# A hybrid decoder block on one core: mixer weight sums at other steps, the fifth product's sums through two buffers, feed-forward sums on GpSimd

## The chip, the core and the metric

The kernel runs on one core of a Trainium2 chip. The core has a matrix engine (TensorE, PE in the profile; PEld is its loading of weights), a vector engine (VectorE, DVE), a scalar engine (ScalarE, ACT), a general engine (GpSimd, POOL) and SyncE (SP), which here issues nearly all transfers between DRAM and the on-chip memory SBUF. TensorE writes its results into PSUM banks. Every engine works through its own list of instructions in a fixed order, and an instruction waits on semaphores until its operands are there. An instruction that waits holds up all that stands behind it on its engine, transfers that SP issues included.

The metric is the device time of one execution in microseconds (us).

## What is computed

The block works on 1024 tokens of width 1024, in float32. A state-space branch and an attention branch read one normalised input, are gated and merged, and go through one output projection. Then come a cross-attention into 256 memory tokens, a SwiGLU feed-forward part of hidden width 2816, and a last norm.

```python
u = rms_norm(h, norm_mix[l])
proj = u @ w_in[l]
...
h = h + (gate_a * out_a + gate_b * out_b) @ w_mix_out[l]
h = h + memory_cross_attention(rms_norm(h, norm_mem_q[l]), rms_norm(mem, norm_mem_kv[l]),
                               w_mem_q[l], w_mem_kv[l], w_mem_o[l])
f_a, f_b = jnp.split(rms_norm(h, norm_ffn[l]) @ w_ffn_in[l], 2, axis=-1)
h = h + (jax.nn.silu(f_a) * f_b) @ w_ffn_out[l]
return rms_norm(h, norm_final)
```

The change touches the projection by `w_mix_out` and the product by `w_ffn_in`, with the weights prepared for the first while the state-space branch runs.

## The kernel before

Every matmul operand is held as two rounded parts, high and low. `B.split` (L177, L178) makes them: ScalarE copies the source to the high part, and VectorE (or GpSimd, where its last argument says so) subtracts to get the low part. A product of two such operands is three matmuls per step: high by high, high by low, low by high.

Large products are done by a seven-product scheme on 2 x 2 blocks: instead of eight block products there are seven, of sums of blocks. The operands of the left side are named A11, A12, A22 (blocks) and S1 to S4 (sums of blocks); the weights' sums are made in the same way. A name with h or l at the end is a high or low part: S4h, S4l.

The text names three places in the program.

**The state-space stage** (`stage_ssm`) runs a list of 32 gate products, `gates`, and hangs other work on their numbers through the dictionary `todo`. Four groups of states, q = 0 to 3, hang on gates 4 + 7q and the following ones: `turn_weights`, `states`, `toeplitz` (a strip built by doubling in the buffer Ts), `out`. xg is the load of the states' input from DRAM. On the same list hang the sums of the mixer weights, k = 0 to 3: `mix_fetch` loads two row blocks of `w_mix_out` into two buffers mw, `mix_sums` makes four sums on VectorE (L501), and `mix_store` writes them to the DRAM array sums_d (L505). Before the change these three hang on gates 7k, 7k + 2 and 7k + 3.

**The mixer** (in `stage_tail`) runs seven products by n in the order 1, 2, 6, 5, 3, 7, 4, each in four row groups `mix_mm(n, i)`, and adds each result into the hidden rows H (`mix_add`, L622, the tiles h in the profile). So product 5, with operand S1, is the fourth in this order, and product 3, with operand S4, is the fifth. The sums S4 lie in DRAM (s_d in the profile). `mix_s4(kk)` loads one half into a buffer with the tag xs, of which there is one, and `give` splits it into S4h and S4l. Beside the products a list `side` prepares the first two panels of the feed-forward weights: wpr is the raw panel, wph and wpl its high and low part, and the sums between them are made on GpSimd (L694 to L699). The gain of the next norm is spread over the partitions by `bcast_gain` into a buffer gbc, of which there is one too. `scaled` scales a token block for that norm: the sum of squares, `rsqrt` with a power on GpSimd (L196), its refinement rt and r on VectorE (L200 to L202), and xs = h x r x gain (L216).

**The feed-forward start.** `norm_blocks(t)` does the same for the eight token blocks t = 0 to 7, turns the scaled block with TensorE (L222, into banks misc and pv), and makes the operands. For t below 4 the turned block is stored to x_d and split into A11 and A12. For t = 4 to 7 the stored block comes back as xa, ScalarE copies the second half to sx, and VectorE makes s (for S3), the first half of sx (for S1), then two more sums in xa (L880 for S2, L881 for S4). `put` splits S2, S3 and S1; the fourth sum and A22 go to r_d and come back in `norm_rest` as xr. The products of the first panels, `start(0)`, `start(1)`, `middle(0)` and so on, call `prod` (L962). The second panel's `start(1)` uses A11 and A12 with weights whi and wlo from w_d; the first that reads S2 is `middle(0)`.

A scheduler with a cost model puts every engine's instructions in order when the program is built, so that the order of the lists is not that of the code.

Of the kernel before, what the change touches and what calls it, by code (L numbers as in the profile page):

```python
# [9 lines left out]
F32 = mybir.dt.float32  # L10
# [4 lines left out]
ALU = mybir.AluOpType  # L15
# [4 lines left out]
P = 128  # L20
D = 1024
# [435 lines left out]
def stage_ssm(B, s5, qp, uT, w_in, gate_d, u_d, y_d, w_mix_out, sums_d):  # L457

    A, S = B.A, B.S
    s5.qp = qp  # L460
    w = {}

    def gate_weights(p):

        w[p] = [B.wblock(w_in, 4 * n, 4, C_G + 256 * p, 256) for n in range(2)]

    def gate(j, h):
        if h == 0 and j % 2 == 0 and j < 14:
            gate_weights(j // 2 + 1)
        ps = B.bank()  # L470
        o = j % 2 * P
        for k in range(8):
            wh, wl = [t_[:, k % 4, o:o + P] for t_ in w[j // 2][k // 4]]
            B.mm3(ps, wh, wl, *uT.rhs(k, h), k == 0, k == 7)
        gs = qp.tile([P, 512], F32, tag="gs", bufs=2, name="gs")
        mark.append(A.activation(gs, ps, AF.Sigmoid))
        A.dma_start(gate_d[j * P:(j + 1) * P, 512 * h:512 * h + 512], gs)

    def toeplitz():
        with B.tc.issue_after(mark[-1].ins):  # L480
            s5.toeplitz()

    def weights(q):
        with B.tc.issue_after(s5.doubled.ins):
            s5.weights(q)

    mw = {}

    def mix_fetch(k):
        mw[k] = [qp.tile([P, D], F32, tag="mw", bufs=2, name="mw") for _ in range(2)]  # L490
        for w_, r_ in zip(mw[k], (k, 4 + k)):
            S.dma_start(w_, w_mix_out[r_ * P:(r_ + 1) * P, :])

    def mix_parts(k):
        (b11, b12), (b21, b22) = [(w_[:, :512], w_[:, 512:]) for w_ in mw[k]]
        return (5, b11, b12), (7, b12, b22), (6, b22, b11), (4, b21, b22)

    def mix_sums(k):

        for _, o, i in mix_parts(k):  # L500
            B.V.tensor_add(o, o, i)  # L501

    def mix_store(k):
        for n, o, _ in mix_parts(k):
            S.dma_start(sums_d[n, k // 2][:, k % 2 * 512:k % 2 * 512 + 512], o)  # L505

    mark = []
    gates = [lambda j=j, h=h: gate(j, h) for j in range(16) for h in range(2)]
    gate_weights(0)
    s5.weights(0)  # L510
    todo = {}
    for q in range(4):
        todo[4 + 7 * q] = [lambda q=q: s5.turn_weights(q)]
        todo[5 + 7 * q] = [lambda q=q: s5.states(q, u_d)] + ([lambda q=q: weights(q + 1)] if q < 3 else [])
        todo[8 + 7 * q] = [toeplitz]
        todo[9 + 7 * q] = [lambda q=q: s5.out(q), lambda q=q: s5.store(q, y_d)]
    for k in range(4):
        for i, f in ((7 * k, mix_fetch), (7 * k + 2, mix_sums), (7 * k + 3, mix_store)):
            todo.setdefault(i, []).append(lambda f=f, k=k: f(k))
    for i, f in enumerate(gates):  # L520
        for g in todo.get(i, []):
            g()
        f()


def stage_tail(B, big, s2, sh, x, glu, aT, gate_d, kv_d, sums_d, w_fox_o, w_mix_out, g_mq, w_mem_q, w_mem_o, g_ffn,
               w_ffn_in, w_ffn_out, g_fin, out):
    nc, V, A, G, T, S, small, ident = B.nc, B.V, B.A, B.G, B.T, B.S, B.small, B.ident
# [18 lines left out]
    fox, part, xm, mixw, msets, late = {}, {}, {}, {}, [], []  # L547
# [6 lines left out]
    def give(name, mk, k, src):  # L554
        B.split(*[a[k // 2][:, k % 2, :] for a in operand(name, mk)], src)
# [93 lines left out]
    H = [bslot(name=f"h{t}") for t in range(NT)]  # L649
    for t in range(NT):  # L650
        S.dma_start(H[t], x[t * P:(t + 1) * P, :])
    gq = B.bcast_gain(s2, g_mq)
    u2 = Act(s2, "t", NS2, 8, L, name="u2")

    xss = {}

    def scaled(t):
        xss[t] = tmp("xs")
        B.norm_scale(xss[t], H[t], B.rstd(H[t]), gq)

    def turned(t, banks):
        B.norm_turn(xss.pop(t), u2, t, banks)
# [54 lines left out]
        return [fetch, plain, sums, seventh, rest]  # L717

    def mix_s4(kk):
        y = s2.tile([P, D], F32, tag="xs", bufs=1, name="s4")  # L720
        S.dma_start(y, s3_d[kk])
        for k in range(2):
            give("S4", bslot, 2 * kk + k, y[:, 512 * k:512 * k + 512])

    side = [f for j in range(AHEAD_IN) for f in ahead(j)]
    side[6:6] = [lambda kk=kk: mix_s4(kk) for kk in range(2)]
    mix_weights(6)
    for i in range(4):
        mix_add(1, i)
    for n, m in ((2, 5), (6, 3), (5, 7), (3, 4), (7, None), (4, None)):  # L730
        for i in range(4):
            mix_mm(n, i)
            if n == 7:
                turned(i, ("mm", "misc"))
            mix_add(n, i)
            if n in (3, 4):
                scaled((n == 4) * 4 + i)
            elif late:
                late.pop()()
            elif side:  # L740
                side.pop(0)()
        if m:
            mix_weights(m)

# [101 lines left out]
            comb[name] = [[mk(F32R, f"{name}{s}").rearrange("p (k c) -> p k c", k=2) for _ in range(2)] for s in "hl"]  # L846
        return comb[name]

    def put(name, mk, i, src, neg=False):

        hi_, lo_ = blocks(name, mk)
        for kk in range(2):
            sv = src[:, kk * 256:(kk + 1) * 256].rearrange("p (k c) -> p k c", k=2)
            hi, lo = [a[kk][:, :, i * P:(i + 1) * P] for a in (hi_, lo_)]
            if neg:
                A.activation(hi, sv, AF.Copy, scale=-1.0)
                V.scalar_tensor_tensor(out=lo, in0=sv, scalar=-1.0, in1=f32(hi), op0=ALU.mult, op1=ALU.subtract)
            else:
                B.split(hi, lo, sv)

    def norm_blocks(t):
        i = t % 4
        xs = s2.tile([P, D], F32, tag="xs", bufs=1, name="xs")
        B.norm_scale(xs, H[t], B.rstd(H[t]), gf)
        S.dma_start(h_d[t], H[t])
        ps = [B.turn(xs, b, ("misc", "pv")[b]) for b in range(2)]
        if t < 4:
            for b in range(2):
                xf = sh.half("xf")
                A.copy(xf, ps[b])  # L870
                S.dma_start(x_d[i][:, 512 * b:512 * b + 512], xf)
                put(("A11", "A12")[b], slot, i, xf)
            return
        xa, sx, s3 = tmp("xa"), tmp("sx"), sh.half("s3")
        S.dma_start(xa, x_d[i])
        a11, a12, s1n, a22 = xa[:, :512], xa[:, 512:], sx[:, :512], sx[:, 512:]
        A.copy(a22, ps[1])
        V.tensor_sub(s3, a11, ps[0])
        V.tensor_sub(s1n, ps[0], a22)
        V.tensor_sub(a11, s1n, a11)  # L880
        V.scalar_tensor_tensor(out=a12, in0=a11, scalar=-1.0, in1=a12, op0=ALU.mult, op1=ALU.subtract)  # L881
        put("S2", slot, i, a11)
        put("S3", bslot, i, s3)
        put("S1", bslot, i, s1n, neg=True)
        S.dma_start(r_d[i][:, :512], a12)
        S.dma_start(r_d[i][:, 512:], a22)

    def norm_rest(i):
        y = tmp("xr")
        S.dma_start(y, r_d[i])  # L890
        put("S4", bslot, i, y[:, :512])
        put("A22", bslot, i, y[:, 512:])

    raws, wts, ev = {}, {}, {}
# [163 lines left out]
    for j in range(2, NF):  # L1058
# [7 lines left out]
        f = w_fetch(j + 2) if j + 2 < NF else f  # L1066
# [840 lines left out]
```

## Time and profile before

| | us |
|---|---|
| runs | 1604.41, 1609.55, 1599.38 |
| median of the runs | 1604.41 |
| profiled execution, its own time | 1599.39 |
| span of the profiled execution | 1597.6 |
| mean granted TensorE clock | 0.981 of full |

A row of a timeline reads: start in us, length in us, engine, line, operation, output<-input, shapes, and how often in a row; in square brackets stands the idle time of the engine before it and what ended it. A row of the waits reads: engine and line that waited, what it waited for, then us in total, times, longest us. SPq is SyncE's queue issuing transfers.

The stages that the change touches lie, by the names in the timeline, from 130 to 200 us (the first group of states), from 750 to 805 us (the mixer's last products) and from 940 to 975 us (the feed-forward start).

### The profile page before, as it was taken

To read this page: it belongs to the slowest core of one execution; us is meant where nothing else is said; L and a number is where in the kernel's file an instruction comes from. 1 tells how busy PE (TensorE), PEld (TensorE's weight loads), DVE (VectorE), ACT (ScalarE), POOL (GpSimd) and SP (SyncE) were. 2 spreads that over 40 slices of the span, in tenths; PEclk is the share of its full clock that TensorE was granted. 3 is DMA by queue.
4 is the path that set the end of the run, shared out by engine and by line. 5 is a ranking of instruction groups with operands and counts; after the bars stand their busy time and mean duration, and the time that the engine had idled before them with its cause. 6 is when DMAs were issued, how large, how long until landed. Compare 5 with 4: busy or idle time off the path is not lost.

```text
span 1597.6 us, 20547 instructions
## 1 busy us (share of the span) xinstructions
PE 1533.2 (96%) x7301; PEld 1260.2 (79%) x7301; DVE 1069.6 (67%) x1886; ACT 671.1 (42%) x1191; POOL 266.1 (17%) x337
## 2 busy tenths in 40 slices
PE   5899899999999899999899989999999999999997
PEld 5688788898777668887688778888888888788885
DVE  5757666435687777778775687777677776565455
ACT  5522343422566554223455565333333333344342
POOL 3014434110121123213201200010000000000001
PEclk8899999999999999999999999999999999999998
DMA  8747745652032736557732177445544554796642
GB/s 268 147 95 172 229 124 103 135 175 31 1 68 43 164 101 184 198 178 279 243 105 93 53 262 271 158 156 161 168 156 152 162 161 148 278 391 212 196 152 106
DMA packets 202872, 258.71 MB, mean 162 GB/s; under 512 B 36025, under 2 KB 127065, under 8 KB 202257
## 3 DMA queue, kind: packets, MB, share of 16 engines
q1 hardware_dynamic: 196144, 241.67, 50.3%
q10 hardware_dynamic: 6624, 15.73, 2.6%
q8 instruction: 57, 0.93, 0.2%
q14 instruction: 47, 0.38, 0.1%
HBM read 176.08 MB, written 83.20 MB: 162 GB/s over the span
## 4 chain that ended last, share of the span: by engine, by line
PE 78%; DVE 8%; DMA 5%; POOL 3%; issue 3%; ACT 2%; SPq 1%; DVEq 0%; ACTq 0%; POOLq 0%
PE mm L962 15%; PE pv L962 7%; PE mm L167 7%; PE mm L168 7%; PE mm L169 7%; PE mm L1099 4%; PE sc L962 4%; PE sc L1099 3%; PE pv L1099 3%; PE sc L167 2%; PE sc L169 2%; PE sc L168 2%; PE misc L1099 1%; PE pv L167 1%; PE pv L169 1%
## 5 line engine op out<-in xcount | busy, mean ns | idle before, releaser
L178 DVE TENSOR_TENSOR wlo<-raw,whi 128x1024 fp32r<-128x1024 f32 (+2 forms) x126 | 134.8, 1072 | 113.9 <-ACT whi L177 113.5
L177 ACT CAST whi<-raw 128x1024 fp32r<-128x1024 f32 (+2 forms) x127 | 115.6, 914 | 140.7 <-PE mm L168 43.6
L167 PE MATMUL mm<-uh,whi 128*128 128x512 f32 x344 | 139.6, 406 | 1.9 <-ACT whi L177 1.8
L169 PE MATMUL mm<-uh,wlo 128*128 128x512 f32 x344 | 137.0, 399 | 0.5 <-DVE wlo L178 0.5
L168 PE MATMUL mm<-ul,whi 128*128 128x512 f32 x344 | 137.1, 398 | 0.0
L178 DVE TENSOR_TENSOR ol<-or,oh 128x1024 fp32r<-128x1024 f32 x73 | 89.4, 1224 | 70.8 <-ACT oh L177 69.6
L177 ACT CAST oh<-or 128x1024 fp32r<-128x1024 f32 x73 | 76.8, 1053 | 103.4 <-PE mm L1099 34.9
L994 POOL TENSOR_TENSOR g<-a,c 128x512 f32<-128x512 f32 x22 | 35.6, 1618 | 392.6 <-ACT a L993 392.6
L1726 POOL TENSOR_TENSOR pl<-pf,ph 128x512 fp32r<-128x512 f32 (+1 forms) x32 | 39.5, 1234 | 244.7 <-DVE ph L1725 198.1
L169 PEld LDWEIGHTS mm<-uh,wlo 128*128 128x128 f32 x344 | 66.0, 192 | 15.2 <-DVE wlo L178 1.5
L167 PEld LDWEIGHTS mm<-uh,whi 128*128 128x128 f32 x344 | 66.4, 193 | 14.6 <-ACT whi L177 2.3
L168 PEld LDWEIGHTS mm<-ul,whi 128*128 128x128 f32 x344 | 66.2, 193 | 11.2
L196 POOL TENSOR_TENSOR r<-ms,mhalf 128x1 f32<-128x1 f32 (+1 forms) x30 | 20.6, 690 | 309.2 <-DVE ms L192 280.4
L1723 ACT ACTIVATE pf<-sc 128x512 f32<-128x512 f32 (+1 forms) x96 | 46.5, 490 | 48.5 <-DVE sc L1719 28.6
L962 PE MATMUL pv<-S3h,we 128*128 128x512 f32 x176 | 58.1, 389 | 0.0
L1729 DVE TENSOR_TENSOR pl<-pf,ph 128x512 fp32r<-128x512 f32 (+2 forms) x64 | 35.6, 558 | 10.5 <-ACT ph L1728 9.4
L1099 PE MATMUL mm<-ol,oh 128*128 128x512 f32 x106 | 41.2, 389 | 0.0
L1099 PE MATMUL mm<-oh,ol 128*128 128x512 f32 x106 | 41.2, 389 | 0.0
L1099 PE MATMUL mm<-oh 128*128 128x512 f32 x106 | 41.2, 389 | 0.0
L1194 POOL TENSOR_TENSOR sg<-sg,ga 128x512 f32<-128x512 f32 x16 | 28.8, 1821 | 72.8 <-DVE sg L1187 72.8
L167 PE MATMUL mm<-yh,whi 128*128 128x512 f32 x104 | 40.9, 393 | 0.0
L167 PE MATMUL sc<-uh,whi 128*128 128x512 f32 x104 | 40.8, 393 | 0.0
(680 smaller groups left out, 4610.7 us busy)
## 6 DMA issues: line engine op xcount, KB each, us to landing
or<-c_d SPq DMA_DIRECT2D x77, 256.0 KB
wo<-in_w_ffn_out_dram SPq DMA_DIRECT2D x22, 512.0 KB
c_d<-g SPq DMA_DIRECT2D x44, 256.0 KB
t_d<-wo SPq DMA_DIRECT2D x44, 256.0 KB
or<-t_d SPq DMA_DIRECT2D x44, 256.0 KB
raw<-in_w_ffn_in_dram SPq DMA_DIRECT2D x20, 512.0 KB
rawb<-in_w_ffn_in_dram SPq DMA_DIRECT2D x20, 512.0 KB
raw<-in_w_in_dram SPq DMA_DIRECT2D x18, 512.0 KB
```

Of the source, the lines that this page charges most:

```text
L167: T.matmul(ps, lh, rh, start=first, stop=False)
L168: T.matmul(ps, lh, rl, start=False, stop=False)
L169: T.matmul(ps, ll, rh, start=False, stop=last)
L177: self.A.copy(hi, src)
L178: (self.G if pool_lo else self.V).tensor_sub(lo, src, f32(hi))
L962: T.matmul(ps, l_[:, k, :], r_, start=first and k == 0 and i == 0, stop=k == 3 and i == 2, skip_group_check=True)
L994: G.tensor_mul(g[:, 512:], a1, c1)
L1099: T.matmul(ps, l_[:, gi], r_[:, 512:], start=n < 3 and p == 0 and k == 0 or n == 7 and p == 0 and k == 0, stop=p == NP - 1 and k == 2, ski ...
L1194: self.B.G.tensor_mul(self.out[j][:, cs], self.out[j][:, cs], ga)
L1723: self.exp = A.activation(pf[:, off:], ps[:, off:], AF.Exp)
L1726: G.tensor_sub(pl[:, off:], pf[:, off:], f32(ph[:, off:]))
L1729: V.tensor_sub(pl[:, off:], pf[:, off:], f32(ph[:, off:]))
```

## The change

1. `mix_fetch`, `mix_sums` and `mix_store` hang on gates 10 + 5k, 12 + 5k and 13 + 5k instead of 7k, 7k + 2 and 7k + 3.
2. The two halves of S4 are loaded into two buffers, with the tags xs and gbc, and their parts go to `slot` buffers (those that A11 had for the first product) instead of `bslot`. The pieces in `late` and the two loads are now the head of the list `side`. The gain of the norm, which uses gbc, is loaded after product 6.
3. In `norm_blocks`, for t = 4 to 7, the third and fourth sums are made on GpSimd. The fourth is a plain addition, and its sign is put right later, where S4 is split with `neg=True`. S2 is split last, and its low part on GpSimd.

```diff
-        for i, f in ((7 * k, mix_fetch), (7 * k + 2, mix_sums), (7 * k + 3, mix_store)):
+        for i, f in ((10 + 5 * k, mix_fetch), (12 + 5 * k, mix_sums), (13 + 5 * k, mix_store)):
...
-    gq = B.bcast_gain(s2, g_mq)
...
-    xss = {}
+    xss, gq = {}, []
...
-        B.norm_scale(xss[t], H[t], B.rstd(H[t]), gq)
+        B.norm_scale(xss[t], H[t], B.rstd(H[t]), gq[0])
...
-        y = s2.tile([P, D], F32, tag="xs", bufs=1, name="s4")
+        y = s2.tile([P, D], F32, tag=("xs", "gbc")[kk], bufs=1, name="s4")
...
-            give("S4", bslot, 2 * kk + k, y[:, 512 * k:512 * k + 512])
+            give("S4", slot, 2 * kk + k, y[:, 512 * k:512 * k + 512])
...
-    side[6:6] = [lambda kk=kk: mix_s4(kk) for kk in range(2)]
+    side[:0] = late + [lambda kk=kk: mix_s4(kk) for kk in range(2)]
...
-            elif late:
-                late.pop()()
             elif side:
                 side.pop(0)()
+        if n == 6:
+            gq.append(B.bcast_gain(s2, g_mq))
...
-    def put(name, mk, i, src, neg=False):
+    def put(name, mk, i, src, neg=False, low=V):
...
-                B.split(hi, lo, sv)
+                B.split(hi, lo, sv, low is G)
...
-        V.tensor_sub(a11, s1n, a11)
-        V.scalar_tensor_tensor(out=a12, in0=a11, scalar=-1.0, in1=a12, op0=ALU.mult, op1=ALU.subtract)
-        put("S2", slot, i, a11)
+        G.tensor_sub(a11, s1n, a11)
+        G.tensor_add(a12, a11, a12)
         put("S3", bslot, i, s3)
         put("S1", bslot, i, s1n, neg=True)
+        put("S2", slot, i, a11, low=G)
...
-        put("S4", bslot, i, y[:, :512])
+        put("S4", bslot, i, y[:, :512], neg=True)
```

How the scheduled order moves, at three places. The lines of the changed kernel are one lower than before from L653 on. First SP's list in the state-space stage. Before, from the last two u_d stores of the projection on:

```order
L440 DMA u_d<-us 128x8x128
L153 DMA raw<-in_w_in_dram 128x4x256
L492 DMA mw<-in_w_mix_out_dram 128x1024 x2
L1450 DMA xg<-u_d 128x1024
L505 DMA sums_d<-mw 128x512 x3
L492 DMA mw<-in_w_mix_out_dram 128x1024
L505 DMA sums_d<-mw 128x512 x2
L492 DMA mw<-in_w_mix_out_dram 128x1024
L153 DMA raw<-in_w_in_dram 128x4x256 x2
L1439 DMA Ts<-Ts 112x128
```

The changed kernel from the same place:

```order
L440 DMA u_d<-us 128x8x128
L153 DMA raw<-in_w_in_dram 128x4x256
L1449 DMA xg<-u_d 128x1024
L492 DMA mw<-in_w_mix_out_dram 128x1024 x2
L505 DMA sums_d<-mw 128x512 x4
L492 DMA mw<-in_w_mix_out_dram 128x1024 x2
L153 DMA raw<-in_w_in_dram 128x4x256
L505 DMA sums_d<-mw 128x512
L153 DMA raw<-in_w_in_dram 128x4x256
L1438 DMA Ts<-Ts 112x128
```

The first xg load has moved ahead of the first two fetches, and the fourth store of the first group ahead of the second group's fetches. From the copy of Ts with 96 partitions on, SP's list is the same in both.

Second, VectorE's list in the mixer, from the first panel's wpl on to the first h of the fifth product's successor. The rows h<-h,mm and h<-h,misc at the start are the sums of product 5. Before:

```order
L178 TENSOR_TENSOR wpl<-wpr,wph 128x1024
L178 TENSOR_TENSOR S4l<-s_7202,S4h 128x512 x2
L622 TENSOR_TENSOR h_6964<-h_6964,mm 128x512
L622 TENSOR_TENSOR h_6965<-h_6965,mm 128x512
L178 TENSOR_TENSOR wpl<-wpr,wph 128x512
L178 TENSOR_TENSOR wph<-wpr,wph 128x512
L622 TENSOR_TENSOR h_6966<-h_6966,misc 128x512
L178 TENSOR_TENSOR wlo<-raw,whi 128x1024
```

The changed kernel:

```order
L178 TENSOR_TENSOR wpl<-wpr,wph 128x1024
L622 TENSOR_TENSOR h_6964<-h_6964,mm 128x512
L622 TENSOR_TENSOR h_6965<-h_6965,mm 128x512
L178 TENSOR_TENSOR wpl<-wpr,wph 128x512
L178 TENSOR_TENSOR wlo<-raw,whi 128x1024
L178 TENSOR_TENSOR wpl<-wpr,wph 128x512
L622 TENSOR_TENSOR h_6966<-h_6966,misc 128x512
```

The two S4l have left this place (all four now stand together ahead of product 5's sums), and the sum of the misc bank has moved behind a weight split and behind the second wpl of 128x512. On SP, the load of the gain now stands between the two loads of product 3's weights, ahead of the next panel's wpr.

Third, GpSimd's list at the feed-forward start. r_8941, r_9024 and r_9075 are the powers for the token blocks t = 5, 6 and 7. Before, with the end of the list of norms and what follows:

```order
L196 TENSOR_TENSOR r_8854<-ms_8853,mhalf 128x1
L196 TENSOR_TENSOR r_8941<-ms_8940,mhalf 128x1
L196 TENSOR_TENSOR r_9024<-ms_9023,mhalf 128x1
L196 TENSOR_TENSOR r_9075<-ms_9074,mhalf 128x1
L994 TENSOR_TENSOR g<-a_9222,c_9248 128x512
```

The changed kernel:

```order
L196 TENSOR_TENSOR r_8941<-ms_8940,mhalf 128x1
L879 TENSOR_TENSOR xa<-sx,xa 128x512
L196 TENSOR_TENSOR r_9024<-ms_9023,mhalf 128x1
L880 TENSOR_TENSOR xa<-xa 128x512
L178 TENSOR_TENSOR S2l<-xa,S2h 128x2x128 x2
L879 TENSOR_TENSOR xa<-sx,xa 128x512
L880 TENSOR_TENSOR xa<-xa 128x512
L178 TENSOR_TENSOR S2l<-xa,S2h 128x2x128 x2
L196 TENSOR_TENSOR r_9075<-ms_9074,mhalf 128x1
L879 TENSOR_TENSOR xa<-sx,xa 128x512
```

The groups of t = 4 and t = 5 now stand among the powers, that of t = 5 ahead of the power for t = 7; the groups of t = 6 and t = 7 follow. On TensorE the turns of t = 7 into pv have moved directly behind those of t = 6, and its turns into misc behind the first product of the second panel.

## The prediction

> **What bounds the kernel now.** I read the page first, then TensorE's waits over the whole span, then windows around them, and last the timelines of the engines that these waits name. The page:
>
> ```profile
> span 1597.6 us, 20547 instructions
> PE 1533.2 (96%) x7301; PEld 1260.2 (79%) x7301; DVE 1069.6 (67%) x1886; ACT 671.1 (42%) x1191; POOL 266.1 (17%) x337
> ```
>
> TensorE is busy for 1533.2 of 1597.6 us, so 64.4 us are idle, and no part of the change removes a matmul. All that the change can win is idle time of TensorE and the slow clock behind it. Its waits, longest first where the change touches them:
>
> ```profile
> PE mm L615 <- ACT S4h L177: 3.5, 1, 3.5
> PE misc L222 <- DVE rt L201: 3.1, 1, 3.1
> PE pv L1426 <- ACT m L1504: 2.3, 1, 2.3
> PE pv L1500 <- ACT Tt L1444: 2.0, 1, 2.0
> PE misc L222 <- DVE u2l L178: 1.2, 1, 1.2
> PE misc L222 <- DVE h L622: 1.0, 1, 1.0
> PE mm L962 <- DMA whi<-w_d: 0.9, 1, 0.9
> PE mm L615 <- DVE S4l L178: 0.7, 1, 0.7
> PE pv L1457 <- DMA xg<-u_d: 0.7, 1, 0.7
> ```
>
> L1426, L1500 and L1457 are the first group of states (5.0 us), S4h and S4l are the fifth product (4.2), rt and whi the feed-forward start (4.0). The windows give the clock behind them (columns: window, length, busy time of PE, PEld, DVE, ACT and POOL with counts, granted clock, DMA share, GB/s):
>
> ```profile
> 190.00:193.00 3.00, 3.00 (x11) 2.52 (x11) 2.97 (x4) 0.96 (x2) 2.42 (x4) 0.50 0.99 267
> 777.00:780.00 3.00, 2.28 (x6) 1.63 (x6) 3.00 (x4) 0.85 (x2) 2.92 (x3) 0.50 0.22 91
> 958.00:961.00 3.00, 2.71 (x9) 2.32 (x10) 3.00 (x6) 2.06 (x8) 0.00 (x0) 0.50 0.80 285
> ```
>
> Behind each of the three places the clock is 0.50 for a while. As an estimate from how far the windows of half clock reach, it lasts 3.4 us in the first place and 6.8 us in each of the others, and costs half of that: 1.7, 3.4 and 3.4 us. If everything went, it would be 13.2 + 8.5 = 21.7 us.
>
> **Part A, mixer weight sums later.** The work is the same, only its place in the queues moves. These rows are SP's and VectorE's around the first group of states:
>
> ```profile
> 139.08 6.49 SPq L505 DMA_DIRECT2D sums_d<-mw  x2
> 143.58 1.64 DVE L501 TENSOR_TENSOR mw<-mw 128x512 f32<-128x512 f32 x1
> 145.66 0.38 SPq L492 DMA_DIRECT2D mw<-in_w_mix_out_dram  x1
> 186.40 5.02 SPq L505 DMA_DIRECT2D sums_d<-mw  x4
> 191.52 0.57 SPq L1450 DMA_DIRECT2D xg<-u_d  x1
> ```
>
> The order of the instructions shows that the change is far smaller than its numbers: only the first two fetches and stores trade places, and from the 96x256 copy of Ts on SP's queue is as before, with the third and fourth groups of stores still ahead of the xg load at 191.52. So this load still waits for the fourth group. What can come earlier is the second fetch, which stood at 145.66 behind a store that waited for the sum at 143.58: it is freed when the first group is done, some 1 to 3 us earlier. VectorE's first sum meanwhile goes behind two other operations of 0.69. I put A at -1.5 us. Its ends are -3 (the second fetch fully earlier, and the wait at L1426 below what slows the clock) and +1.5 (a store that now waits ahead of the scan).
>
> **Part B, S4 through two places.** Rows of the fifth product before, with the waits that decide it:
>
> ```profile
> 764.02 0.68 DVE L178 TENSOR_TENSOR S4l<-s,S4h 128x512 fp32r<-128x512 f32 x1
> 764.73 4.00 SPq L721 DMA_DIRECT2D s<-s_d  x1
> 774.69 0.62 ACT L177 CAST S4h<-s 128x512 fp32r<-128x512 f32 x1 [1.86 <-DMA s<-s_d]
> 775.36 0.50 PE L615 MATMUL mm<-whi,S4h 128*128 128x512 f32 x1 [3.50 <-ACT S4h L177]
> 772.86 1.22 DVE L178 TENSOR_TENSOR wpl<-wpr,wph 128x1024 fp32r<-128x1024 f32 x1 [2.87 <-ACT wph L177]
> 775.44 1.73 POOL L695 TENSOR_TENSOR wpr<-wpr 128x512 f32<-128x512 f32 x1
> 778.81 1.27 POOL L698 TENSOR_TENSOR wpr<-wpr 128x512 f32<-128x512 f32 x1
> 775.95 1.76 DVE L178 TENSOR_TENSOR S4l<-s,S4h 128x512 fp32r<-128x512 f32 x1
> 777.64 1.27 DVE L622 TENSOR_TENSOR h<-h,mm 128x512 f32<-128x512 f32 x2
> 781.16 0.67 DVE L622 TENSOR_TENSOR h<-h,misc 128x512 f32<-128x512 f32 x1
> 786.51 0.39 PE L615 MATMUL misc<-whi,S4h 128*128 128x512 f32 x1
> ```
>
> The second half's load could start only at 764.73, when S4l had read the shared buffer, and landed for the cast at 774.69. With a second place both loads stand together on SP, ahead of the next weights, and the operands lie in buffers free since product 1. So the 3.5 + 0.7 us go, and the half clock with them: -7.6.
>
> Three costs come in. First, four S4l of 0.68 and two h sums now stand on VectorE ahead of the second weight split of the fourth product, and that weight's load stands behind the two S4 loads: 4 x 0.68 of new work, of which a good third is not hidden, +1.0. Second, the h sum at 781.16 moves behind the split of a GpSimd weight sum. That sum ends at 778.81 + 1.27 = 780.1, 7.2 us after wpl at 772.86; a cast of 0.62, the split 0.68 and the sum 0.67 make 9.2. The load under wpl stands on SP behind the gain's load, which now waits for the last S4l; against that it no longer shares the queues with the load of 764.73. So I leave wpl near 772, and the bank is free at 781 to 782. TensorE, 6.6 us earlier than 786.51, wants it at 779.9: a wait of 1 to 2 us, +1.5. Third, VectorE is the neighbour that is late next: in the window from 777 to 780 it is busy 3.00 of 3.00 us; its queue becomes 2.4 us shorter (two S4l gone), while TensorE would come 5 us earlier, so the waits on h and u2l grow by about 2: +2. A longer wait can bring the half clock back. The gain's load moved behind the sixth product is read at the first xs, long after: nothing, and if it landed late, it would show as a wait of xs. B: -7.6 + 1.0 + 1.5 + 2 = -3.1, between -7.6 (no cost) and +1 (second and third costs end above 2.3 us and bring 3.4 us of half clock).
>
> [...]
>
> **Part C, sums and S2 splits to GpSimd.** For each of four token blocks VectorE loses two sums and two S2 splits. The rows:
>
> ```profile
> 954.03 1.28 DVE L216 SCALAR_TENSOR_TENSOR xs<-h,r,gbc 128x1024 f32<-128x1024 f32 x1
> 957.44 1.28 DVE L216 SCALAR_TENSOR_TENSOR xs<-h,r,gbc 128x1024 f32<-128x1024 f32 x1
> 959.57 0.69 DVE L880 TENSOR_TENSOR xa<-sx,xa 128x512 f32<-128x512 f32 x1
> 966.83 0.76 DVE L178 TENSOR_TENSOR S2l<-xa,S2h 128x256 fp32r<-128x256 f32 x2
> 961.29 0.49 PE L962 MATMUL mm<-A11h,wlo 128*128 128x512 f32 x1
> 968.47 0.39 PE L962 MATMUL mm<-S2l,whi 128*128 128x512 f32 x1
> 955.46 1.09 PE L222 MATMUL misc<-ident,xs 128*128 128x128 f32 x4 [3.12 <-DVE rt L201]
> L694 POOL TENSOR_TENSOR wpr<-wpr 128x512 f32<-128x512 f32 x2 | 2.6, 1278 | 25.5 <-DVE wpl L178 25.5
> L1726 POOL TENSOR_TENSOR pl<-pf,ph 128x256 fp32r<-128x256 f32 x8 | 5.9, 736 | 166.2 <-DVE ph L1725 119.6 <-DVE rc L1760 46.6
> L994 POOL TENSOR_TENSOR g<-a,c 128x512 f32<-128x512 f32 x22 | 35.6, 1618 | 392.6 <-ACT a L993 392.6
> ```
>
> VectorE saves 2 x 0.69 + 0.76 = 2.1 us a block. On GpSimd the same costs 2 x 1.28 + 2 x 0.74 = 4.0 us, or 2 x 1.62 + 2 x 0.74 = 4.7 where it meets VectorE. So xs of the seventh block, at 954.03 before, comes about 3 to 4 us earlier and the 3.1 us go. But the eighth block's rstd now stands on GpSimd behind the sixth block's group. That group can begin when the sixth block's second sum, which now stands behind that xs, is done, at about 951.5; it ends at 955.5 to 956.5, the rstd half a us later, and xs of the eighth block (1.28, and a sum of 0.69 ahead of it) at about 959.2 against 957.44 + 1.28 = 958.7 before. TensorE, free at 955.46 - 3.12 = 952.3, has done the seventh block's turns by 953.2 and by its new order turns the eighth ahead of the second panel's products: it stands for 6 us there, and the half clock remains. The seventh block's two sums follow on VectorE, then the misc turns at 960.6. The products that ran at 961.29 come at about 962.3, with the two matmuls that used to run earlier: +1.0.
>
> Then S2l of the last block, done at 966.83 + 0.76 = 967.6 before, is GpSimd's last of two groups that start at 960.5: 968.5 at 4.0 a group, and 972.9 at 6.2, that is 4.7 and VectorE's four S3l and S1l (2 x 0.76) in the way. For those read two operands in SBUF, as did the S4l at 775.95, which took 1.76 beside GpSimd's L695 instead of 0.68. TensorE would read S2l at 968.47 + 1.0 = 969.5, so it waits 0 to 3.4 us. Nothing in the trace says which; I take the middle, 1.7: C = +1.0 + 1.7 = +2.7. The ends are -2 (eighth rstd not late, S2l in time) and +9 (S2l at 974.5, a wait of 5, and 3.4 of half clock again). S2l last and S4 negated cost nothing: the same instruction shapes, and S4's product is read hundreds of matmuls later.
>
> [...]
>
> **Sum.** -1.5 - 3.1 + 2.7 = -1.9 us, against the profiled execution's 1599.4 (result file; its span is 1597.6): 1597.5. That execution is the lowest of the three runs, 5.0 below their median of 1604.4. I add half of this, 2.5, for a median of new runs: 1600.
>
> **Rivals.** (1) The three waits go and nothing takes their place in B and C: -1.5 - 7.6 - 7.4 = -16.5, 1599.4 - 16.5 + 2.5 = 1585. For it: VectorE is only 67% busy. Against it: the new order puts an older wait behind GpSimd. (2) GpSimd sets the feed-forward start: S2l of the last block at 973.1 makes C +4.6, which takes up A and B together; at 974.5 with the half clock C is +9, and 1599.4 - 1.5 - 3.1 + 9 + 2.5 = 1606, slower than before. For it: 1.62 to 1.73 us a sum beside VectorE. Against: VectorE loses 2.1 us a block there, so meets it less. (3) A and B do not do what they say: the mixer sums barely move (A 0), and the wait on S4h becomes one on the h sum's bank with its half clock (B +1): 1599.4 + 1 + 2.7 + 2.5 = 1606. For it: the order on SP. Against: VectorE has 2.9 us idle ahead of wpl.
>
> **How the numbers follow.** Forecast 0.53, (1) 0.15, (2) 0.20, (3) 0.12. Forecast and (2), (3) run from 1594 to 1610 with their bounds; (1) reaches down to 1583. The range 1587 to 1610 leaves out part of (1) and little above. Faster by over 1% (below 1588.4, the least that a measurement here can tell from none) needs most of (1): 0.09. Slower by over 1% (above 1620.4) needs more than every bound, 0.02; within 1%: 0.89.
>
> **What would show it.** A: the order of fetches, and L1426's wait at 1 to 2.5 us. B: no wait on S4h, one on a bank or split near 780 and longer ones on h or u2l. C: no wait on rt at the seventh block, one of about 6 us ahead of the eighth block's pv turns, and one ahead of the first S2l. A clock of 1.00 from 777 to 784 and from 954 to 961 with no new waits would prove me wrong towards (1); any wait over 5 us on S2l towards (2).

## The result, and the profile after

| | before | after |
|---|---|---|
| median of 18 runs each, us | 1604.02 | 1609.88 |
| lowest and highest, us | 1599.38, 1609.55 | 1603.51, 1618.67 |
| profiled execution, its own time, us | 1599.39 | 1612.03 |
| its mean granted TensorE clock | 0.981 | 0.979 |

The ratio is 1.0036, with an interval from 1.0022 to 1.0050. On 1604 us that is 5.8 us more, between 3.5 and 8.0. The forecast was 1600.0, 4 us less than before's median. So 1609.88 lies just inside the range of 1587 to 1610, but the time went the other way: it rose by 5.8 us where 4 less were forecast. Rivals (2) and (3), both at 1606, come nearest. The two profiled executions differ by 12.6 us, twice as much as the medians, since before's is its lowest run and after's one of its longer ones; places are read from the traces, and sizes from the runs.

The page of the changed kernel, its span and its busy times:

```profile
span 1610.3 us, 20551 instructions
PE 1539.8 (96%) x7301; PEld 1265.1 (79%) x7301; DVE 1071.1 (67%) x1870; ACT 670.9 (42%) x1191; POOL 282.9 (18%) x353
```

VectorE has 16 instructions fewer than before and GpSimd 16 more, as the diff says: two sums and two splits for each of four blocks. Yet VectorE's busy time did not fall; it rose from 1069.6 to 1071.1. Sixteen removed operations ought to have taken four times 2.1 us off it. This line alone, read against the one of before, already says that other VectorE operations became longer.

TensorE's waits in the changed kernel (us in total, times, longest), those of the three places:

```profile
PE pv L222 <- DVE xs L216: 6.2, 1, 6.2
PE misc L615 <- DVE h L622: 2.6, 1, 2.6
PE mm L615 <- DVE h L622: 2.2, 2, 1.4
PE pv L1456 <- DMA xg<-u_d: 2.2, 1, 2.2
PE misc L222 <- DVE h L622: 2.2, 1, 2.2
PE pv L1499 <- ACT Tt L1443: 2.1, 1, 2.1
PE mm L961 <- POOL S2l L178: 1.3, 1, 1.3
PE pv L961 <- ACT S3h L177: 1.1, 1, 1.1
```

Every wait that the change was aimed at is gone from this list: S4h, S4l, rt, whi, and L1426 too, of which the prediction had left 1 to 2.5 us. In each place others stand there instead: 4.3 us for 5.0 in the first group of states, 7.0 for 6.4 in the mixer (with h and u2l of the turns), 9.0 for 4.0 in the feed-forward start (with a short wait on S2h, 0.4).

To see where the time went, the start of the same matmul is taken in both traces, and the difference after minus before noted:

| place, us in before | after minus before, us |
|---|---|
| 165, ahead of the first group of states | +0.2 |
| 210, behind it | +0.9 |
| 735, ahead of the mixer's last products | +1.2 |
| 785, the fifth product | -3.9 |
| 800 | +3.4 |
| 815, behind the mixer | +2.0 |
| 951, ahead of the feed-forward start | +2.4 |
| 962 | +4.7 |
| 972 | +9.5 |
| 1360, behind the panels' products | +10.0 |
| 1390 | +12.3 |

The first group of states and the mixer give 0.8 us each. The feed-forward start gives 7.6, from 951 to 1360. Another 2 to 3 us come near 1380, where a wait on c is 2.7 us instead of 1.8; no line of the change touches this code.

The clock in the changed kernel (window, length, busy times with counts, granted clock, DMA share, GB/s):

```profile
172.00:174.00 2.00, 2.00 (x11) 2.00 (x11) 0.00 (x0) 0.00 (x0) 1.69 (x7) 0.50 0.00 1
199.00:201.00 2.00, 2.00 (x10) 1.90 (x9) 1.97 (x3) 1.25 (x4) 0.00 (x0) 0.50 0.18 63
786.00:788.00 2.00, 2.00 (x7) 1.51 (x6) 1.66 (x3) 1.61 (x3) 0.00 (x0) 0.50 1.00 399
962.00:965.00 3.00, 2.92 (x11) 2.25 (x11) 3.00 (x5) 2.00 (x7) 1.95 (x2) 0.50 1.00 403
```

All three places still have a stretch of half clock: a new wait, of 2.1 to 6.2 us, took the place of the old one, and a clock of 0.50 stands behind it. The first group of states has two, behind the wait on Tt and behind that on xg. By the clock records of the two traces, half clock lasts 6.8 us between 750 and 820 us in both kernels, and between 940 and 990 us 6.8 before and 10.2 after, the last 3.4 of them from 976.8 on.

Last, the feed-forward start in the changed kernel's timeline (start, length, engine, line, operation; the wait in brackets):

```profile
954.04 1.83 DVE L178 TENSOR_TENSOR S3l<-s,S3h 128x256 fp32r<-128x256 f32 x2
955.79 2.35 DVE L856 SCALAR_TENSOR_TENSOR S1l<-sx,S1h 128x256 fp32r<-128x256 f32 x2
958.06 0.20 DVE L192 TENSOR_SCALAR ms<-ss 128x1 f32<-128x1 f32 x1
956.95 1.77 POOL L178 TENSOR_TENSOR S2l<-xa,S2h 128x256 fp32r<-128x256 f32 x2
958.68 0.55 POOL L196 TENSOR_TENSOR r<-ms,mhalf 128x1 f32<-128x1 f32 x1
960.36 1.28 DVE L216 SCALAR_TENSOR_TENSOR xs<-h,r,gbc 128x1024 f32<-128x1024 f32 x1
961.79 1.08 PE L222 MATMUL pv<-ident,xs 128*128 128x128 f32 x4 [6.21 <-DVE xs L216]
957.01 0.32 SPq L884 DMA_DIRECT2D r_d<-xa  x1
957.87 0.44 SPq L908 DMA_DIRECT2D whi<-w_d  x1
962.95 0.29 PEld L961 LDWEIGHTS mm<-A11h,whi 128*128 128x128 f32 x1 [0.48 <-DMA whi<-w_d]
965.76 0.32 SPq L884 DMA_DIRECT2D r_d<-xa  x1
966.13 0.42 SPq L874 DMA_DIRECT2D xa<-x_d  x1
970.70 0.69 DVE L877 TENSOR_TENSOR s<-xa,misc 128x512 f32<-128x512 f32 x1 [3.81 <-DMA xa<-x_d]
972.07 1.40 POOL L879 TENSOR_TENSOR xa<-sx,xa 128x512 f32<-128x512 f32 x1 [4.58 <-DVE sx L878]
974.85 1.78 POOL L178 TENSOR_TENSOR S2l<-xa,S2h 128x256 fp32r<-128x256 f32 x2
975.80 0.50 PE L961 MATMUL mm<-S2l,whi 128*128 128x512 f32 x1 [1.35 <-POOL S2l L178]
```

The same transfers on SP in before:

```profile
951.87 0.45 SPq L909 DMA_DIRECT2D whi<-w_d  x1
958.89 0.45 SPq L875 DMA_DIRECT2D xa<-x_d  x1
961.22 0.32 SPq L885 DMA_DIRECT2D r_d<-xa  x1
```

Three readings. Ahead of the 6.2 us wait, VectorE's queue is full: two pairs of splits take 1.83 and 2.35 us, and ms, the first step of the eighth block's rstd, stands behind them until 958.06. And behind the wait the eighth block's xa comes late: its load on SP, at 966.13, stands behind a store of xa that waits for GpSimd's sum, and VectorE idles 3.81 us for it. GpSimd idles 4.58 us in its turn, until VectorE has made sx. In before the load was issued at 958.89, ahead of that store. Third, the weights of the second panel are late in the same way: their load is issued at 957.87, behind a store at 957.01 that waits for the sum that GpSimd ends at 956.99, where before it stood at 951.87. That is 6.0 us later, 3.6 more than the 2.4 of the whole trace, and the first product behind the 6.2 us wait still waits for it, until 962.95. The rows of S1l's splits in both kernels, from the view of one tile (minimum, median and maximum in ns), before:

```profile
L857 DVE SCALAR_TENSOR_TENSOR S1l<-sx,S1h x8: 420/423/427, 945.4 to 967.8; 128x256 fp32r<-128x256 f32 x8
```

and after:

```profile
L856 DVE SCALAR_TENSOR_TENSOR S1l<-sx,S1h x8: 414/1186/1501, 947.9 to 975.1; 128x256 fp32r<-128x256 f32 x8
```

The same eight instructions, whose code is not changed, take a median of 1186 ns instead of 423.

### The profile page after: what moved, and what is told of

It reads as the page before. It is cut to its first block, busy times and chain, and to the rows that moved or that the text cites. A ratio compares the mean times of both kernels' runs of the same rounds, so it can differ in the third digit from the quotient of the medians.

```text
span 1610.3 us, 20551 instructions
## 1 busy us (share of the span) xinstructions
PE 1539.8 (96%) x7301; PEld 1265.1 (79%) x7301; DVE 1071.1 (67%) x1870; ACT 670.9 (42%) x1191; POOL 282.9 (18%) x353
## 4 chain that ended last, share of the span: by engine, by line
PE 76%; DVE 8%; DMA 5%; POOL 4%; issue 3%; ACT 2%; SPq 1%; DVEq 0%; POOLq 0%; ACTq 0%
PE mm L961 14%; PE pv L961 7%; PE mm L167 7%; PE mm L168 7%; PE mm L169 7%; PE mm L1098 4%; PE sc L961 3%; PE sc L1098 3%; PE pv L1098 3%; PE sc L167 2%; PE sc L169 2%; PE sc L168 2%; PE misc L1098 1%; DMA or<-in_w_ffn_out_dram 1%; PE pv L615 1%
## 5 line engine op out<-in xcount | busy, mean ns | idle before, releaser
L167 PEld LDWEIGHTS mm<-uh,whi 128*128 128x128 f32 x344 | 65.8, 191 | 14.4 <-ACT whi L177 2.3
```

The lines of the kernel that those rows point to most:

```text
L167: T.matmul(ps, lh, rh, start=first, stop=False)
```

## The experiments

Ratios are to the kernel before, run on the same chip in the same batch; us are worked out as the ratio's distance from 1 times 1604. A stands for the mixer sums at later steps, B for S4 through two places, C for the feed-forward sums and splits on GpSimd.

### Each part alone, and A with B

`e1_a` is before with the numbers of the mixer sums changed:

```diff
-        for i, f in ((7 * k, mix_fetch), (7 * k + 2, mix_sums), (7 * k + 3, mix_store)):
+        for i, f in ((10 + 5 * k, mix_fetch), (12 + 5 * k, mix_sums), (13 + 5 * k, mix_store)):
```

> Only the mixer weight sums at the later gates. Theory (the feed-forward part carries the loss): within 1.5 us of before; the wait at the turns of L1426 (2.3 us) goes and the wait on the xg load grows from 0.7 to some 2.2 us, as in the changed kernel's trace. Rival (the loss is spread over the three parts): +2 us or more.

Measured: 1600.72 us, ratio 0.9984 (0.9966 to 1.0002), so -2.6 us (-5.5 to +0.3). The wait at L1426 is gone; Tt (2.5) and xg (0.6) remain, so xg's wait did not grow to 2.2 as was expected, and Tt's did by 0.5. A does what was said; that it gains is likely, not shown.

`e2_b` is before with the second part alone:

```diff
-        y = s2.tile([P, D], F32, tag="xs", bufs=1, name="s4")
+        y = s2.tile([P, D], F32, tag=("xs", "gbc")[kk], bufs=1, name="s4")
...
-    side[6:6] = [lambda kk=kk: mix_s4(kk) for kk in range(2)]
+    side[:0] = late + [lambda kk=kk: mix_s4(kk) for kk in range(2)]
```

> Only S4 through two places, with the gain loaded later. Theory: 0 to +2 us against before; no wait on S4h, but waits on the hidden rows' sums (h) of 2 to 3 us each in their place. Rival (the mixer carries the loss): +4 us or more.

Measured: 1606.70 us, ratio 1.0024 (1.0009 to 1.0039), so +3.9 us (+1.4 to +6.3). B alone is slower. TensorE's waits in the mixer of `e2_b`:

```profile
PE misc L222 <- DVE h L622: 2.8, 1, 2.8
PE misc L615 <- DVE h L622: 2.7, 1, 2.7
PE mm L615 <- DVE h L622: 1.8, 1, 1.8
```

The waits on S4h and S4l (4.2) are gone, and three on sums of h (7.3) stand there. By places, this trace loses only 0.4 us between 735 and 815, though; 2.3 are lost ahead of 735, where B changes nothing, and 2.9 near 1380. Where the runs' 3.9 us come from isn't shown by it.

`e3_c` is before with the third part alone:

```diff
-        V.tensor_sub(a11, s1n, a11)
-        V.scalar_tensor_tensor(out=a12, in0=a11, scalar=-1.0, in1=a12, op0=ALU.mult, op1=ALU.subtract)
-        put("S2", slot, i, a11)
+        G.tensor_sub(a11, s1n, a11)
+        G.tensor_add(a12, a11, a12)
...
+        put("S2", slot, i, a11, low=G)
```

> Only the feed-forward sums and S2's low parts on GpSimd. Theory: +5 to +9 us against before, with a wait of some 6 us of TensorE ahead of the eighth block's turns and the eighth block's xa load landing some 5 us late. Rival (the mixer carries the loss): at most +2 us.

Measured: 1611.79 us (6 runs), ratio 1.0053 (1.0034 to 1.0072), so +8.5 us (+5.5 to +11.5). The waits are those of the whole change, 6.2 on xs and 1.3 on S2l; in the trace 5.8 us are lost between 951 and 1360. In the same stretch kernels whose feed-forward start is as before differ from before by 0.1 to 1.7 us (`e2_b`, `e9_ab_n2`, `e1_a`, `e4_ab`), so places in single traces are no better known than that.

`e4_ab` is the whole change without the third part.

> The first two parts together, the feed-forward start as before. Theory: -1 to +2 us against before, the sum of the two alone. Rival (the mixer carries the loss): +4 to +6 us.

Measured: 1603.50 us, ratio 0.9994 (0.9979 to 1.0009), so -1.0 us (-3.4 to +1.4). C is thus what makes the whole slower. The fifth product's last bank in `e4_ab`, by start:

```profile
778.16 2.31 DVE L178 TENSOR_TENSOR wlo<-raw,whi 128x1024 fp32r<-128x1024 f32 x1
779.47 2.12 POOL L698 TENSOR_TENSOR wpr<-wpr 128x512 f32<-128x512 f32 x1
781.62 1.14 ACT L177 CAST wph<-wpr 128x512 fp32r<-128x512 f32 x2 [3.71 <-POOL wpr L698]
782.27 0.69 DVE L178 TENSOR_TENSOR wpl<-wpr,wph 128x512 fp32r<-128x512 f32 x1 [1.80 <-ACT wph L177]
782.88 0.68 DVE L622 TENSOR_TENSOR h<-h,misc 128x512 f32<-128x512 f32 x1
783.62 0.50 PE L615 MATMUL misc<-whi,S4h 128*128 128x512 f32 x1 [3.47 <-DVE h L622]
```

This is the chain that the prediction wrote down, sum, cast, split, h sum, bank. Only its sum is longer: GpSimd's addition met a VectorE split and took 2.12 us, not 1.27, and it began 0.7 us later. So the bank is free at 783.6, not 781 to 782, and the wait is 3.5 us, not 1.5.

The three parts alone add up to -2.6 + 3.9 + 8.5 = +9.8, and A with B and C alone to +7.5; the whole is +5.8 (+3.5 to +8.0). With some 3 us on each these agree.

### Why C costs: the load, the power, or VectorE's longer splits

The reason that the prediction gave for the 6 us wait was that the eighth block's power stands on GpSimd behind the sixth block's group. The trace offered two others: the load behind the store, and VectorE's longer splits. `e5_c_xa` is C with each block's xa load issued ahead of the store of the block before:

```diff
-        S.dma_start(xa, x_d[i])
...
+        if t < 7:
+            xas[t + 1] = tmp("xa")
+            S.dma_start(xas[t + 1], x_d[i + 1])
```

> The feed-forward part alone, but each block's xa load is issued on SP ahead of the store of the block before, which waits for GpSimd. Theory (the last block's load stands behind a store that waits for GpSimd's sum, and makes S2's low part late): the eighth xa load lands 4 to 5 us earlier, the waits on S3h, S2h and S2l (2.8 us together) go, and the time is 3 to 4 us below that of the part alone, +4 to +5.5 us against before. Rival (GpSimd's own sums and splits set S2l): less than 1 us is won.

Measured: 1608.07 us, ratio 1.0001 (0.9984 to 1.0019), so +0.2 us (-2.6 to +3.0; by the medians +2.6). The wait on xs and the row of s in this kernel:

```profile
PE pv L222 <- DVE xs L216: 6.8, 1, 6.8
```

```profile
959.87 0.42 SPq L891 DMA_DIRECT2D xa<-x_d  x1
961.39 0.68 DVE L882 TENSOR_TENSOR s<-xa,misc 128x512 f32<-128x512 f32 x1
```

The load of the eighth block stands at 959.87 again, and no wait for a load is left, but the wait on xs is as long as ever. In the trace the feed-forward start loses 2.9 us instead of the 5.8 of `e3_c`. So the load behind the store cost about 3 us in these traces, and by the runs, 8.5 against 0.2, some 8, with about 4 us of doubt. The weights' load is not mended by this edit: it still stands behind a store that waits for GpSimd, and is 3.7 us later than in before when the trace's own shift of 3.4 is taken off.

`e6_c_rv` is C with the eighth block's rsqrt on VectorE, by iteration, so that it meets no queue of GpSimd:

```diff
-        B.norm_scale(xs, H[t], B.rstd(H[t]), gf)
+        B.norm_scale(xs, H[t], B.rstd(H[t], t < 7), gf)
```

> The feed-forward part alone, with the eighth block's power made by Newton steps on VectorE instead of GpSimd, so that it doesn't stand behind the sixth block's sums. Theory (the power's place costs about 2 us): the wait of 6.2 us ahead of the eighth block's turns falls to 2 to 4 us and the time by 2 to 3 us, to +5.5 to +6.5 us against before, the last block's load being late still. [...]

Measured: 1612.33 us, ratio 1.0039 (1.0024 to 1.0054), so +6.3 us (+3.9 to +8.7). The wait on xs is still there:

```profile
PE pv L222 <- DVE xs L216: 6.7, 1, 6.7
```

```profile
956.61 2.35 DVE L857 SCALAR_TENSOR_TENSOR S1l<-sx,S1h 128x256 fp32r<-128x256 f32 x2
958.88 0.20 DVE L192 TENSOR_SCALAR ms<-ss 128x1 f32<-128x1 f32 x1
```

Here the theory fell, although the time is in its range: without the power on GpSimd the wait stays, because its input ms is itself late, behind VectorE's own splits. The substitute isn't free: from the end of ms to r it takes 2.0 us, where the way over GpSimd takes 1.6 in `e3_c`. The rows of the changed kernel say the same: ms is done at 958.26 and the power starts at 958.68, so GpSimd's group held it for 0.4 us.

`e7_c_xarv` has both edits.

> Both mends together. Theory (the two queues make all of the loss): within 2 us of before. Rival (GpSimd's slower work makes it): +5 us or more against before.

Measured: 1607.94 us, ratio 1.0018 (1.0004 to 1.0032), so +2.9 us (+0.6 to +5.1), with a wait of 7.3 us on xs. That is between the theory and the rival. In the trace 3.3 us are lost between 951 and 1360, so something beside the late xa and the power was left.

`e8_c_low` puts the sums back on VectorE and leaves only S2's low part on GpSimd:

```diff
-        V.scalar_tensor_tensor(out=a12, in0=a11, scalar=-1.0, in1=a12, op0=ALU.mult, op1=ALU.subtract)
-        put("S2", slot, i, a11)
+        V.tensor_add(a12, a11, a12)
...
+        put("S2", slot, i, a11, low=G)
```

> The feed-forward part with both sums back on VectorE, only S2's low parts on GpSimd: no store waits for GpSimd and all powers stand ahead of the splits. Theory: -2 to +2 us against before. Rival (a GpSimd operation beside VectorE's is what costs): +4 us or more.

Measured: 1605.33 us, ratio 1.0000 (0.9985 to 1.0015), as the theory had it. The wait on xs falls to 3.0 us. GpSimd's pair of splits is longer than in the changed kernel:

```profile
954.85 2.37 POOL L178 TENSOR_TENSOR S2l<-xa,S2h 128x256 fp32r<-128x256 f32 x2 [3.46 <-ACT S2h L177]
```

So both engines are slowed here: two splits, counted at the 0.74 that one takes at L1726 in before, take 2.37 on GpSimd, and beside them VectorE's rt at 955.85 takes 0.70 us instead of 0.15, while S1l's pair at 955.18 keeps its 0.76.

`e13_idle_pool` asks for the price of the meeting itself. It is before, with four sums on GpSimd in each of the blocks t = 4 to 7 that nothing reads:

```diff
+        dz = s2.tile([P, 512], F32, tag="dz", bufs=1, name="dz")
+        for w_ in (512, 512, 256, 256):
+            G.tensor_add(dz[:, :w_], s1n[:, :w_], gf[:, :w_])
```

> The kernel before with four GpSimd sums per block (two 128x512, two 128x256, of operands in SBUF, whose results nobody reads) added where the change puts its GpSimd work; VectorE keeps all of its own work. Theory (GpSimd's work lengthens VectorE's operations beside it): VectorE's S3l, S1l and S2l pairs take 1.8 to 2.4 us instead of 0.76, the eighth block's scaled xs comes 2 us or more later, and the time is +1 to +5 us against before. Rival (only the queues cost, the contention is hidden): within 1 us of before, the pairs at 0.8 us.

Measured: 1615.21 us (6 runs), ratio 1.0065 (1.0040 to 1.0090), so +10.4 us (+6.4 to +14.4), above the +1 to +5 of the theory. Rows of VectorE and GpSimd in this kernel:

```profile
951.92 1.77 DVE L881 SCALAR_TENSOR_TENSOR xa<-xa 128x512 f32<-128x512 f32 x1
955.69 1.80 DVE L857 SCALAR_TENSOR_TENSOR S1l<-sx,S1h 128x256 fp32r<-128x256 f32 x2
953.11 0.99 POOL L196 TENSOR_TENSOR r<-ms,mhalf 128x1 f32<-128x1 f32 x1
957.42 0.15 DVE L200 TENSOR_TENSOR rt<-r 128x1 f32<-128x1 f32 x1
960.49 1.09 PE L222 MATMUL misc<-ident,xs 128*128 128x128 f32 x4 [7.47 <-DVE rt L201]
```

VectorE has exactly its work of before, and TensorE's wait on rt grows from 3.1 to 7.5 us. The sum that took 0.69 takes 1.77, and S1l's pair 1.80 instead of 0.76. The power is done at 954.1, yet rt, next in its chain, starts on VectorE at 957.42: the queue there is late, not the power. Work on GpSimd that nothing waits for costs as much as the whole change, or more; the intervals overlap. This shows that the meeting alone can cost time. It isn't the price in C: GpSimd works 5.0 us a block here and 4.5 in the changed kernel, and VectorE keeps its two sums, one of which takes 1.77 us beside GpSimd instead of 0.69.

`e14_c_sums_xa` is `e5_c_xa` with S2's low part back on VectorE, so that only the sums are on GpSimd.

> Of the feed-forward part the two sums on GpSimd, S2's low parts on VectorE, with the xa loads ahead of the stores. Theory (contention is what is left, and less of it with 2.6 us of GpSimd work a block than with 4.1): 0 to +2 us against before, the wait ahead of the eighth block's turns 3 to 5 us instead of 6.8. Rival (GpSimd's splits are harmless): as with the splits on GpSimd, a wait above 6 us.

Measured: 1609.69 us, ratio 1.0024 (1.0005 to 1.0044), so +3.9 us (+0.8 to +7.1). The wait on xs was to fall to 3 to 5 us and is 6.3, as the rival said; S1l's pairs still take 1.8. So the two sums alone are enough for the wait, with VectorE's queue as full; the store that waits for them is there too, and the weights' load behind it is 3.4 us later than in before. That this version is slower than `e5_c_xa` isn't shown; the intervals overlap.

### B: can its new waits be mended?

`e9_ab_n2` is A and B with two empty steps ahead of the last four of the list, so that the second panel's sums come later:

```diff
+    at = len(side) - 4
+    side[at:at] = [lambda: None] * 2
```

> The first two parts, with the second panel's split and sums two steps later in the list beside the mixer's products, so that the sum of the misc bank no longer stands behind the splits of GpSimd's sums. Theory (S4's wait became this wait): the wait of 3.5 us on h ahead of the misc bank's product falls below 1 us, and the time to -2 to -6 us against before, that is 1 to 5 below the two parts as they were. Rival (VectorE as a whole is late there, whatever the order): the wait moves to the next sum and the time stays within 1 us of the two parts.

Measured: 1604.05 us, ratio 0.9994 (0.9974 to 1.0014). The wait of the misc bank is gone, and the next one has grown from 2.1 us:

```profile
PE misc L222 <- DVE h L622: 4.3, 1, 4.3
PE mm L615 <- DVE h L622: 2.5, 2, 1.7
```

The wait moved and was not removed, as the rival had it.

`e10_ab2` is A and B with the list's steps still held back by the late piece of S1:

```diff
+            elif late:
+                late.pop()()
```

> The first two parts, but the two S4 loads stay where they were in the list. Theory: the two places alone remove the wait on S4h, and the same sums of h are late as when the loads come early: -2 to +1 us against before. Rival (putting the loads ahead of everything is what makes the sums late): -4 us or less.

In this kernel one split of S1 is issued a second time, and with it all of `side` comes a step later: the two S4 loads stand together at 755.52, not at 749.96 as in `e4_ab`. The two traces differ in this place by 3.8 us for other reasons, so the loads are some 1.8 us later. That is far less than a return to their old places, 751.63 and 764.73, and does not test the expectation as it was put. Measured: 1605.61 us, ratio 1.0000 (0.9982 to 1.0017). S4's waits stay away, and those on h are 4.2 (two), 4.0 and 1.2, in all 9.4 against 8.1 in `e4_ab`. So the two places remove S4's waits a step later in the list too, and the sums of h are late all the same.

### Versions of the whole

`e11_abc_xa` is the whole change with the xa loads first, as in `e5_c_xa`.

> The whole change, with each block's xa load ahead of the store of the block before. Theory (the late load costs about 3 us wherever it stands): 2 to 5 us below the whole change, 0 to +4 us against before. Rival (that mend worked only beside the old mixer): less than 1 us is won.

Measured: 1605.73 us, ratio 1.0009 (0.9993 to 1.0025), so +1.4 us (-1.1 to +4.0), 4.4 less than the whole change. The wait on S2l falls to 0.2, that on xs stays at 6.8.

`e12_best` is `e9_ab_n2` with `e8_c_low`'s part C and the loads first.

> The first two parts with the later panel sums, and of the feed-forward part only S2's low parts on GpSimd, with the xa loads ahead of the stores. Theory (what cost is gone): -2 to -6 us against before. Rival (GpSimd's splits beside VectorE still cost): 0 to +3 us.

Measured: 1605.38 us, ratio 0.9994 (0.9976 to 1.0013). The gain that was expected isn't there; the waits on xs (4.1) and on h (4.2) are. No version was shown to be faster than before; A alone comes nearest.

## Why the prediction was wrong, point by point

**A, forecast -1.5, measured -2.6 (-5.5 to +0.3).** Right in mechanism, and in size as far as the interval tells. The second fetch came 4.2 us earlier, at 141.46 instead of 145.66, not 1 to 3, and L1426's wait went altogether. The next late thing is xg or Tt, 0.6 to 2.5 us by the run; in the changed kernel (2.1 on Tt, 2.2 on xg) the clock behind each is 0.50.

**B, forecast -3.1, measured alone +3.9 (+1.4 to +6.3).** The waits moved as written: S4's go, and the bank behind the second panel's split and the sums of h take their place. The term that failed is the half clock. The -7.6 counted 3.4 us of it as gone, and it is there as before, 6.8 us long, behind the new waits. Without that term the sum is -4.2 + 4.5 = +0.3; TensorE's waits in the mixer went from 6.4 to 7.0 us, and the changed kernel's trace loses 0.8 there. The "+1.5" was too small as well: the bank's wait is 2.6 to 3.5 in the changed kernel, `e2_b` and `e4_ab`. GpSimd's sum was put at 1.27 us and took 2.12 beside VectorE, in a chain whose every other link came out as written. With A it shows less (-1.0 for both, against -2.6 for A alone), and the intervals don't part these.

**C, forecast +2.7, measured alone +8.5 (+5.5 to +11.5).** Here the sign was lost. The failed step is "Nothing in the trace says which; I take the middle, 1.7: C = +1.0 + 1.7 = +2.7": the wait on S2l was sized by GpSimd's work alone, and the late load of xa that set it was put at nothing. By places in the trace of `e3_c`, the first term, up to 962, is 2.2 us, and the second, from there to 1360, 3.6. In the changed kernel they are 2.3 and 5.3, with one more stretch of half clock.

The second term asked only how long GpSimd's last two groups would be. They took 4.5 and 4.6 us, inside the forecast 4.0 to 6.2. But the last one doesn't follow the one before: GpSimd idles 4.58 us between them, because the eighth block's xa is late. A moved sum drags the store that reads it, and the store holds SP's queue: here the store is issued at 965.76, the load behind it at 966.13. The prediction did not follow r_d to the load of xa behind it, and so put this at nothing. With the loads ahead of the stores, the wait on S2l is 0.4 us (`e5_c_xa`) and 0.2 (`e11_abc_xa`), and the trace loses 2.9 and 3.2 us between 951 and 1360, near the forecast for C. By the runs the three pairs with and without this edit differ by 8.3 (`e3_c`, `e5_c_xa`), 3.4 (`e6_c_rv`, `e7_c_xarv`) and 4.4 us (the whole change, `e11_abc_xa`), each with 3 to 4 us of doubt.

The first term, "+1.0", is 2.0 to 2.7 in the trace of every kernel with the two sums on GpSimd (up to 1.1 where the start is as before). Two things that the prediction left out end close together there. One is contention, which it charged to one engine: it lengthened GpSimd's groups by VectorE's splits, and left VectorE's splits at 2 x 0.76 a block. They took 1.83 + 2.35 = 4.2, that is 2.7 more a block, which more than uses up the 2.1 that VectorE was to save. The row that told it was quoted: S4l at 1.76 instead of 0.68, a VectorE row. In the changed kernel both engines lose: S1l's split on VectorE takes a median of 1186 ns against 423 in before, and GpSimd's pairs of S2l take 1.77 to 1.87 us, counted at 2 x 0.74. By what mechanism they slow each other was not shown. The other is the weights' load, held by a store like xa's. In the changed kernel xs is done at 961.64 and the weights let the first product start at 962.95. Which of the two makes the first term isn't shown: no kernel with the sums on GpSimd has the weights' load ahead of the stores.

The 6 us wait itself came as written, 6.2, and the chain that the prediction named is the one that ends last: GpSimd's group ends at 958.72 and the power starts at 958.68. Less the 2.4 us of shift, xs is done at 959.2, which is the forecast. But VectorE's splits hold ms until 958.26, so the group held the power for only 0.4 us; `e6_c_rv` took the power away, and the wait stayed. That the number came out so well is partly luck.

**The rivals.** Rival (2), slower, with S2l late and C at +9, came true in size: S2l of the last block starts its pair at 974.85 and is done at 976.6; less the 2.4 us by which this trace was late already at 951, that is 974.2, against 974.5 in the rival. Its mechanism did not: S2l is late through the load, not through the length of GpSimd's groups. Against it the prediction set that VectorE "meets it less", with 2.1 us less work a block; the splits that stay on VectorE became 2.7 us longer a block. Rival (3) held for B: the wait became one on the bank, with its half clock.

**The range** held the median by 0.1 us, which is luck; the middles of B and C lay too low.

**Open.** The wait on c near 1380 is 1.8 us in before and in some experiments and 2.7 in after and in others (1.8 to 1.9 in three kernels, 2.3 to 3.1 in thirteen); behind the 2.7 us in after stands half clock from 1383.0 to 1386.4, behind the 1.8 in before none. It costs 2 to 3 us of the profile pair. It goes with the landing of a weight load in code that the change doesn't touch, and what sets that wasn't tried. Of C's cost, the late xa makes 3 to 5 us in the traces and 3 to 8 by the runs. How the rest, 2.6 to 3.3 us in the traces with the loads first, parts into VectorE's longer splits and the late weights wasn't tried.

## What to carry to other kernels

Work moved from VectorE to GpSimd was paid twice in this kernel: S1l's split, which stayed on VectorE, went from a median of 423 ns to 1186. Count what a move does to the operations that stay, with a row where the two engines already meet. Here operations that read one operand from PSUM kept their time, such as h at 0.68 us beside GpSimd's power at 947.35; whether a move pays beside those wasn't tried. When a computation moves to an engine that is slower at it (one sum takes 0.69 us on VectorE in before and 1.28 to 1.40 on GpSimd here), follow every store that reads its result to the queue that issues it, and put the next loads ahead of it. A wait removed was worth here only the distance to the next late thing on the same engine: in the mixer of `e2_b` S4's 4.2 us went, and 7.3 us on h came. Where that left another wait of 2.1 or 2.2 us in the changed kernel, a clock of 0.50 stood behind it.

## What the hardware showed that was not expected

Contention reached small operations too. This VectorE operation on 128 x 1 elements in the changed kernel took 0.69 us; in before the same step took 0.15 to 0.16:

```profile
949.29 0.69 DVE L200 TENSOR_TENSOR rt<-r 128x1 f32<-128x1 f32 x1
```

And half clock followed shorter waits than the 2.3 us that the prediction reckoned with. Behind the 2.1 us wait on Tt the window 172 to 174 has a clock of 0.50 with TensorE busy throughout, and behind the 2.2 us wait on xg the window 199 to 201. In before, the wait of 2.3 us at L1426 has 0.50 behind it from 190 to 193, and the wait of 2.0 us on Tt has none. What length of wait brings it was not shown.
